# An FFN in split fp32: the forms of its inner activations are stored as two parts in place of one

## The chip, the cores and the metric

The kernel runs on one core of a Trainium2 chip, as one program. Its time is the device time of one execution in microseconds (us), the median of several runs. The core has a tensor engine (PE, whose weight loads are listed as PEld), a vector engine (DVE), a scalar engine (ACT), GpSimd (POOL) and SyncE (SP), from whose queue nearly all DMA transfers of this kernel are issued. Each engine carries out its own instructions in the order in which they stand; engines wait for each other by semaphores. The tensor engine runs at one of two clocks, 1.2 or 2.4 GHz; the profile gives the granted clock as a share of the higher one.

## The reference

One layer of a streaming encoder trunk for two streams of 512 and 32 frames, so 544 columns in all, all in fp32. The mixers ahead of the FFN and the last norm are not touched by the change. What matters here is the FFN with its squared relu:

```python
D_MODEL = 2048
D_FF = 4 * D_MODEL
...
h2 = rmsnorm(x, norm2_g[l])
a = jax.nn.relu(jnp.einsum('btd,df->btf', h2, w_ff1[l]))
x = x + jnp.einsum('btf,fd->btd', jnp.square(a), w_ff2[l])
...
y = rmsnorm(x, final_norm_g)
```

## The kernel before

**Two parts.** The tensor engine takes the type fp32r, a shortened fp32. To keep fp32 accuracy, each operand is split into a high part (a cast to fp32r, by ACT) and a low part (the operand less its high part, by DVE), and each product is made of three matmuls: high x high, high x low, low x high (`product`, lines L1145 to L1147). `split_w` (L109, L110) does this for weight tiles; what it makes is a tile `hl`.

**Seven products for eight.** Both FFN products work on 2 x 2 blocks of the matrices with a scheme of seven products. `seven` runs them in the order X, F, X, C, X, D, E, each into a PSUM bank of its own (`bX`, `bF`, `bC`, `bD`, `bE`). X is made three times; the bank is copied by ACT to C, to D (both L1132) and to E (L1134) on the way, so the second product into bX can start only when the copy to bC is done, and the third after the copy to bD. The right operands of the seven products are seven sums and differences of the four blocks of activations, the *forms* (`forms`, L1103 to L1106: t1, t2, t3, t4; the blocks themselves are the other three).

**First product (w1).** 32 rounds (`for i in range(32)`), of 7 x 8 x 3 = 168 matmuls of 128 x 128 by 272 columns. A round loads four 512 KB weight tiles (a11, a21, a22, a12), makes sums of them and splits them. Behind its products, while the next round's products already run, the round's result goes through relu and square (ACT, L1248 to L1253) and the four form sums (DVE), into one tile `ft` of 7 x 272 columns, which goes to DRAM (`hd`, one tensor per chunk of four rounds) as fp32 in one 952 KB store. In rounds 4 to 19 another step stands there too: a tile `xv` of the residual stream is loaded from `x2`, multiplied by the norm's factors on DVE (L1264) and stored back.

**Second product (w2).** Eight chunks of eight turns, 84 matmuls each. A chunk uses the seven forms of four rounds, so seven tiles `hf` with 4 x 272 columns in each of two parts. `load_form` loads one 544 KB form as fp32 into the second half of its tile, casts the high part into the first half (L1192) and subtracts in place (L1193). The seven forms of the next chunk are loaded in turns 1 to 7 of the one before; those of the first chunk during round 32, one after each of its products (`first_forms`), and of these the last two are split only in the course of turn 1 (`late`, `late_split`). A turn takes two weight tiles, r1 and r2, and makes `s12` and `s34`, sums of their halves, each 128 x 1024, split them, and needs s12 from its second product, F, on. F's carry, `accf`, goes through all chunks; the rest of the sums are added to `acc`, whose 16 tiles are loaded from `x2` in the first chunk.

**What sets the order.** PE's instructions stand as the program writes them in the mixers; else the recording layer orders every engine's instructions by priority and dependences, so an edit can move instructions that the source leaves alone. `self.first()` raises the priority of weight loads, splits and bank copies. `self.after` adds an order without a wait: the splits of later chunks' forms were held behind the copy to accf and the last sum of their turn (`hold`).

Of the kernel before, what the change touches and what calls it, by code (L numbers as in the profile page):

```python
# [7 lines left out]
F32 = mybir.dt.float32  # L8
F32R = mybir.dt.float32r
# [7 lines left out]
HALF = 272  # L17
# [21 lines left out]
class Build:  # L39
# [800 lines left out]
    def run(self):  # L840
        tc, nc = self.tc, self.nc
# [4 lines left out]
        dt = lambda n, shape: self.dr.tile(shape, F32, name=n)  # L846
# [4 lines left out]
        self.hd = [dt(f"hd{i}", [128, 7, 4, HALF]) for i in range(8)]  # L851
# [313 lines left out]
    def ffn(self):  # L1165
# [20 lines left out]
        def load_form(ck, f, hold=None, later=None):  # L1186
            t = h_tile("hf")
            r = t[:, 1].bitcast(F32)
            nc.sync.dma_start(r, self.hd[ck][:, f].rearrange("q j t -> q (j t)"))

            def split():
                c0 = a.copy(t[:, 0], r)  # L1192
                c1 = v.tensor_sub(t[:, 1], r, t[:, 0].bitcast(F32))  # L1193
                if hold:
                    self.after(c0, hold[0], "spread")
                    self.after(c1, hold[1], "spread")

            split() if later is None else later.append(split)
            s = lambda k: slice(HALF * k, HALF * k + HALF)
            return [(t[:, 0, s(k)], t[:, 1, s(k)]) for k in range(4)]  # L1200

        w2 = d["w2"]
        nxt, raws, late = [], [], []

        def first_forms(i):

            nxt.append(load_form(0, i, None, late if i > 4 else None))
            if i == 0:

                self.rings["w"] = [0, self.rings["w"][1][-2::-1]]  # L1210
            if i in (0, 3):
                raws.append(self.load_raw(w2[0, len(raws)]))

        for i in range(32):
# [41 lines left out]
            nc.sync.dma_start(self.hd[ck][:, :, j], ft)  # L1256
# [22 lines left out]

        def late_split(i):  # L1280
            if i in (3, 4):
                late.pop(0)()

        for ck in range(8):
            cur, nxt = nxt, []
            for i in range(8):
# [65 lines left out]
                C, E, D, X, F = self.seven(left, cur, 4, accf[:, i] if ck else None, late_split if ck == i == 0 else lambda p: None)  # L1352
                h0 = a.copy(accf[:, i], F)
                if ck == 7:
                    v.tensor_add(hi, hi, accf[:, i].unsqueeze(1).broadcast_to([128, 2, HALF]))
                for p, o in ((C, lo[:, 0]), (X, hi[:, 1]), (D, hi[:, 0]), (E, lo[:, 1])):
                    h1 = v.tensor_add(o, o, p)
                if ck < 7 and i < 7:
                    nxt.append(load_form(ck + 1, i, (h0.ins.name, h1.ins.name)))
# [153 lines left out]
```

## Time and profile before

| | us |
|---|---|
| median of 3 runs | 2269.75 (2269.53 to 2270.97) |
| the profiled execution | 2272.85 |
| its span, first to last instruction | 2271.1 |
| PE busy | 2227.4, 98% of the span |
| DVE busy | 1807.8, 80% |
| ACT busy | 1284.3, 57% |

The first FFN product runs from 902 to 1569.5 us of the span, the second from there to about 2248. Busy time counts computing instructions only. Matmuls are pipelined: each record lasts some 290 ns, while a new one starts every 126 ns, so progress is read from the starts, and a gap in them from a wait that the timeline shows in brackets, with the instruction that ended it. Times of the timeline are us from the start of the span.

### The profile page before, as it was taken

The numbers are of one execution on the slowest core, as the hardware profiler recorded it, in microseconds if no ns is written. First come the engines' busy times: TensorE is split into PE (matmuls) and PEld (weight loads), VectorE is DVE, ScalarE is ACT, GpSimd is POOL, SyncE is SP. The second block draws the span as 40 slices with busy tenths as digits, with TensorE's granted clock in tenths as the row PEclk, the third lists the DMA queues.
The fourth block names the chain that finished last, engine by engine and source line by source line (L and its number), as shares of the span: only waits on it lengthen the run. The fifth ranks groups of instructions, "written<-read, shape, count | busy, mean of one in ns | idle before, by whom it ended". The sixth has DMA issues, their size and how long they took to land.

```text
span 2271.1 us, 46587 instructions
## 1 busy us (share of the span) xinstructions
PE 2227.4 (98%) x19222; PEld 2207.0 (97%) x19222; DVE 1807.8 (80%) x2951; ACT 1284.3 (57%) x2268; POOL 26.6 (1%) x59
## 2 busy tenths in 40 slices
PE   8999999999999999999999999999999999999997
PEld 8999989999999999999999999999999999999997
DVE  7979989877567478777777777777988888888898
ACT  5656666564655256555555555556565565566574
POOL 0000000000000000000000000000000000000000
PEclk9999999999999999999999999999999999999999
DMA  5222222222345565445545444446454244344332
GB/s 196 89 83 93 89 88 83 86 94 75 117 149 179 161 200 173 148 157 178 171 167 178 169 153 151 142 148 241 175 181 162 100 175 162 99 176 163 104 120 98
DMA packets 141317, 322.04 MB, mean 142 GB/s; under 512 B 13360, under 2 KB 68272, under 8 KB 141104
## 3 DMA queue, kind: packets, MB, share of 16 engines
q1 hardware_dynamic: 138928, 316.83, 42.0%
q8 instruction: 150, 2.46, 0.4%
q10 hardware_dynamic: 2176, 2.23, 0.3%
q14 instruction: 63, 0.52, 0.1%
HBM read 262.14 MB, written 56.87 MB: 140 GB/s over the span
## 4 chain that ended last, share of the span: by engine, by line
PE 88%; DVE 7%; ACT 2%; DMA 1%; issue 1%; SPq 0%; DVEq 0%; ACTq 0%
PE g L125 9%; PE bX L1145 8%; PE bX L1146 8%; PE g L127 8%; PE g L126 8%; PE bX L1147 8%; PE bC L1146 3%; PE bD L1146 3%; PE bC L1145 3%; PE bD L1145 3%; PE bF L1145 3%; PE bF L1146 3%; PE bE L1146 3%; PE bE L1145 3%; PE bD L1147 3%; PE bC L1147 3%
## 5 line engine op out<-in xcount | busy, mean ns | idle before, releaser
L125 PE MATMUL g<-a,hl 128*128 128x272 f32 x1648 | 488.0, 296 | 7.2 <-ACT hl L109 6.3
L127 PE MATMUL g<-a,hl 128*128 128x272 f32 x1648 | 477.6, 290 | 1.5 <-DVE hl L110 1.5
L126 PE MATMUL g<-a,hl 128*128 128x272 f32 x1648 | 476.5, 289 | 0.7 <-DVE a L1006 0.7
L110 DVE TENSOR_TENSOR hl<-w,hl 128x1024 fp32r<-128x1024 f32 (+3 forms) x344 | 379.1, 1111 | 121.0 <-ACT hl L109 120.4
L109 ACT CAST hl<-w 128x1024 fp32r<-128x1024 f32 (+3 forms) x344 | 330.6, 961 | 207.4 <-PE g L127 114.6
L110 DVE TENSOR_TENSOR hl<-s,hl 128x1024 fp32r<-128x1024 f32 x256 | 313.1, 1223 | 107.8 <-ACT hl L109 107.7
L109 ACT CAST hl<-s 128x1024 fp32r<-128x1024 f32 x256 | 268.8, 1050 | 177.9 <-PE bD L1147 95.0
L125 PEld LDWEIGHTS g<-a,hl 128*128 128x128 f32 x1648 | 313.3, 190 | 9.6 <-ACT hl L109 6.5
L127 PEld LDWEIGHTS g<-a,hl 128*128 128x128 f32 x1648 | 312.6, 190 | 2.4 <-DVE hl L110 2.4
L126 PEld LDWEIGHTS g<-a,hl 128*128 128x128 f32 x1648 | 312.6, 190 | 1.7 <-DVE a L1006 0.9
L1145 PE MATMUL bX<-hf,hl 128*128 128x272 f32 x768 | 222.5, 290 | 0.5 <-ACT bD L1132 0.5
L1146 PE MATMUL bX<-hf,hl 128*128 128x272 f32 x768 | 222.7, 290 | 0.0
L1146 PE MATMUL bX<-f,hl 128*128 128x272 f32 x768 | 222.6, 290 | 0.0
L1145 PE MATMUL bX<-f,hl 128*128 128x272 f32 x768 | 222.1, 289 | 0.3 <-ACT hl L109 0.3
L1147 PE MATMUL bX<-f,hl 128*128 128x272 f32 x768 | 221.5, 288 | 0.7 <-DVE hl L110 0.7
L1147 PE MATMUL bX<-hf,hl 128*128 128x272 f32 x768 | 221.4, 288 | 0.0
L1145 PEld LDWEIGHTS bX<-hf,hl 128*128 128x128 f32 x768 | 144.8, 189 | 0.9 <-ACT bD L1132 0.7
L1147 PEld LDWEIGHTS bX<-f,hl 128*128 128x128 f32 x768 | 144.6, 188 | 1.0 <-DVE hl L110 1.0
L1145 PEld LDWEIGHTS bX<-f,hl 128*128 128x128 f32 x768 | 144.7, 188 | 0.5 <-ACT hl L109 0.5
L1146 PEld LDWEIGHTS bX<-hf,hl 128*128 128x128 f32 x768 | 144.6, 188 | 0.0
L1147 PEld LDWEIGHTS bX<-hf,hl 128*128 128x128 f32 x768 | 144.5, 188 | 0.0
L1146 PEld LDWEIGHTS bX<-f,hl 128*128 128x128 f32 x768 | 144.4, 188 | 0.0
(437 smaller groups left out, 5731.8 us busy)
## 6 DMA issues: line engine op xcount, KB each, us to landing
w<-w SPq DMA_DIRECT2D x256, 512.0 KB, 3.8
w<-wi SPq DMA_DIRECT2D x76, 512.0 KB, 3.3
hd<-ft SPq DMA_DIRECT2D x32, 952.0 KB, 4.6
hf<-hd SPq DMA_DIRECT2D x56, 544.0 KB, 6.4
w<-wo SPq DMA_DIRECT2D x32, 512.0 KB, 3.8
x<-x SPq DMA_DIRECT2D x32, 272.0 KB, 2.8
hhl<-hh SPq DMA_DIRECT2D x16, 274.0 KB, 3.5
x<-xT SPq DMA_DIRECT2D x16, 272.0 KB, 5.2
```

The costliest lines, as they stand in the source:

```text
L109: self.nc.scalar.copy(hi[:, cols], w[:, cols])
L110: self.last_lo = self.nc.vector.tensor_sub(lo[:, cols], w[:, cols], hi[:, cols].bitcast(F32)).ins.name
L125: te.matmul(o, wh, xh, start=k == 0, stop=False)
L126: te.matmul(o, wh, xl, start=False, stop=False)
L127: te.matmul(o, wl, xh, start=False, stop=k == nk - 1)
L1145: te.matmul(o, wh[:, s], xh, start=start and k == 0, stop=False, skip_group_check=True)
L1146: te.matmul(o, wh[:, s], xl, start=False, stop=False, skip_group_check=True)
L1147: te.matmul(o, wl[:, s], xh, start=False, stop=k == nk - 1, skip_group_check=True)
```

## The change

The forms are split once, in the round that makes them, and stored as two parts. A round casts its whole tile of seven forms to `fh` (ACT, 128 x 1904), subtracts in place (DVE, 128 x 1904) and makes two 952 KB stores, one for each part. `hd` is twice as large. `load_form` is one DMA of 1088 KB and nothing else; the two late splits of the first chunk and the held order of the others go with the splits.

```diff
@@ -848,7 +848,7 @@
         self.ud = [dt(f"ud{i}", [128, 4, NC5]) for i in range(8)]
         self.hh = [dt(f"hh{i}", [128, 4, NC5 - 1]) for i in range(8)]
         self.x2 = [dt(f"x2{i}", [128, T]) for i in range(NK)]
-        self.hd = [dt(f"hd{i}", [128, 7, 4, HALF]) for i in range(8)]
+        self.hd = [dt(f"hd{i}", [128, 7, 2, 4, HALF]) for i in range(8)]
         ones = self.pp.tile([128, 128], F32, name="ones")
         nc.gpsimd.memset(ones, 1.0)
         self.c["ones"] = ones
@@ -1183,28 +1183,18 @@
                 self.hslots.insert(keep, slot)
             return self.hp.tile([128, 2, 4, HALF], F32R, tag=slot, name=n).rearrange("q a k t -> q a (k t)")
-        def load_form(ck, f, hold=None, later=None):
+        def load_form(ck, f):
             t = h_tile("hf")
-            r = t[:, 1].bitcast(F32)
-            nc.sync.dma_start(r, self.hd[ck][:, f].rearrange("q j t -> q (j t)"))
-
-            def split():
-                c0 = a.copy(t[:, 0], r)
-                c1 = v.tensor_sub(t[:, 1], r, t[:, 0].bitcast(F32))
-                if hold:
-                    self.after(c0, hold[0], "spread")
-                    self.after(c1, hold[1], "spread")
-
-            split() if later is None else later.append(split)
+            nc.sync.dma_start(t.bitcast(F32), self.hd[ck][:, f].rearrange("q a j t -> q a (j t)"))
             s = lambda k: slice(HALF * k, HALF * k + HALF)
             return [(t[:, 0, s(k)], t[:, 1, s(k)]) for k in range(4)]
         w2 = d["w2"]
-        nxt, raws, late = [], [], []
+        nxt, raws = [], []
         def first_forms(i):
-            nxt.append(load_form(0, i, None, late if i > 4 else None))
+            nxt.append(load_form(0, i))
             if i == 0:
                 self.rings["w"] = [0, self.rings["w"][1][-2::-1]]
@@ -1253,7 +1243,13 @@
                 a.activation(z, z, AF.Square)
             t = iter((1, 2, 4, 6))
             self.forms((h11, h12, h21, h22), lambda: ft[:, next(t)])
-            nc.sync.dma_start(self.hd[ck][:, :, j], ft)
+
+            fh = tp.tile([128, 7, HALF], F32R, tag="fh", name="fh", bufs=1)
+            fl = ft.bitcast(F32R)
+            a.copy(fh, ft)
+            v.tensor_sub(fl, ft, fh.bitcast(F32))
+            for n, z in enumerate((fh, fl)):
+                nc.sync.dma_start(self.hd[ck][:, :, n, j], z.bitcast(F32))
             if i == 1:
                 self.after(v.tensor_add(self.acc, self.acc, self.rb), last_sum, "start of the products first")
@@ -1276,10 +1272,6 @@
         def end_tile(slot, n):
             t = self.hp.tile([128, 2, 4, HALF], F32R, tag=slot, name=n)
             return t.rearrange("q a k t -> q (a k t)")
-
-        def late_split(i):
-            if i in (3, 4):
-                late.pop(0)()
         for ck in range(8):
             cur, nxt = nxt, []
@@ -1349,14 +1341,14 @@
                     for m in range(2):
                         v.tensor_add(self.acc[:, HALF:T], self.acc[:, HALF:T], sq[:, m])
                     continue
-                C, E, D, X, F = self.seven(left, cur, 4, accf[:, i] if ck else None, late_split if ck == i == 0 else lambda p: None)
-                h0 = a.copy(accf[:, i], F)
+                C, E, D, X, F = self.seven(left, cur, 4, accf[:, i] if ck else None)
+                a.copy(accf[:, i], F)
                 if ck == 7:
                     v.tensor_add(hi, hi, accf[:, i].unsqueeze(1).broadcast_to([128, 2, HALF]))
                 for p, o in ((C, lo[:, 0]), (X, hi[:, 1]), (D, hi[:, 0]), (E, lo[:, 1])):
-                    h1 = v.tensor_add(o, o, p)
+                    v.tensor_add(o, o, p)
                 if ck < 7 and i < 7:
-                    nxt.append(load_form(ck + 1, i, (h0.ins.name, h1.ins.name)))
+                    nxt.append(load_form(ck + 1, i))
                 if ck == 7:
                     for j in range(2):
                         sq = sqt() if i or j else self.acc
```

The change moves instructions that it does not name. The rows below are read as line, operation, out<-in and shape, in the order in which they stand on the engine; line numbers of the second fence of each pair are those of the changed kernel, in which L1239 is L1249 of before (relu), L1243 is L1253 (square), L1293 to L1299 are L1301 to L1307 (the sums to s12 and s34), L1188 is L1189 (load of a form), L1252 is L1256 (the store) and L1308 is L1316 (load of acc).

ACT at the start of a round of the first product, before, from the square of the previous round's h12 on; `bE` is the previous round's last bank and `bC<-bX` is the copy that the round's second X waits for:

```order
L1253 ACTIVATE h_14510<-h_14510 128x272
L1249 ACTIVATE ft<-bE 128x272
L109 CAST hl<-s 128x1024
L1253 ACTIVATE ft<-ft 128x272
L1132 COPY bC<-bX 128x272
L109 CAST hl<-w 128x1024
L109 CAST hl<-s 128x1024
```

The same place after:

```order
L1243 ACTIVATE h_14554<-h_14554 128x272
L1239 ACTIVATE ft<-bE 128x272
L109 CAST hl<-s 128x1024
L1243 ACTIVATE ft<-ft 128x272
L1249 CAST fh<-ft 128x1904
L1132 COPY bC<-bX 128x272
L109 CAST hl<-w 128x1024
```

The new cast of the seven forms stands between the last square and the copy to bC; it does so in all 32 rounds.

DVE at the change-over from the first product to the second, before, from the sum to h12 of round 32 on (`s<-w` and `s<-s,w` of 512 columns are the sums to s12, then to s34):

```order
L1247 TENSOR_TENSOR h_19214<-bD,fsb 128x272
L1301 TENSOR_TENSOR s<-w 128x512
L1193 TENSOR_TENSOR hf<-hf 128x1088
L1302 TENSOR_TENSOR s<-s,w 128x512
L1103 TENSOR_TENSOR ft<-h_19214,ft 128x272
L1105 TENSOR_TENSOR ft<-ft,h_19214 128x272
L1104 TENSOR_TENSOR ft<-ft 128x272
L1306 TENSOR_TENSOR s<-w 128x512
L1106 TENSOR_TENSOR ft<-ft 128x272
L110 TENSOR_TENSOR hl<-s,hl 128x1024
L1307 TENSOR_TENSOR s<-w,s 128x512
```

The same place after:

```order
L1237 TENSOR_TENSOR h_19328<-bD,fsb 128x272
L1103 TENSOR_TENSOR ft<-h_19328,ft 128x272
L1105 TENSOR_TENSOR ft<-ft,h_19328 128x272
L1104 TENSOR_TENSOR ft<-ft 128x272
L1106 TENSOR_TENSOR ft<-ft 128x272
L1250 TENSOR_TENSOR ft<-ft,fh 128x1904
L1293 TENSOR_TENSOR s<-w 128x512
L1298 TENSOR_TENSOR s<-w 128x512
L1294 TENSOR_TENSOR s<-s,w 128x512
L110 TENSOR_TENSOR hl<-w,hl 128x512
L1299 TENSOR_TENSOR s<-w,s 128x512
L110 TENSOR_TENSOR hl<-s,hl 128x1024 x2
```

The sums to s12 stood among the form sums and the splits of loaded forms; now they stand behind all form sums and the new wide subtraction. On PE, turn 1 now runs its product C before its F.

SP at the same change-over, before (`hd_100` holds the forms of the first chunk, `hd_101` those of the second, `hd_107` those of the last; `x_84` and on are tiles of x2):

```order
L89 DMA w<-w 128x1024
L1189 DMA hf<-hd_100 128x1088 x3
L1189 DMA hf<-hd_101 128x1088
L89 DMA w<-w 128x1024
L1189 DMA hf<-hd_101 128x1088 x2
L1256 DMA hd_107<-ft 896x1x272
L89 DMA w<-w 128x1024 x2
L1316 DMA acc_19237<-x_84 128x544
L1316 DMA acc_19237<-x_85 128x544
```

The same place after:

```order
L89 DMA w<-w 128x1024
L1188 DMA hf<-hd_100 128x2176 x3
L1252 DMA hd_107<-fh 896x1x272
L1252 DMA hd_107<-ft 896x1x272
L1188 DMA hf<-hd_101 128x2176
L1308 DMA acc_19355<-x_84 128x544
L1308 DMA acc_19355<-x_85 128x544
L89 DMA w<-w 128x1024
```

The weight tile r2 of turn 2, the second `w<-w` of each fence, stood ahead of the last round's store; now it stands behind both stores, a form and two loads of acc. The tile acc lies in memory that `ft` and `fh` leave.

## Rows read from the trace of the kernel before

**Rows 1.** Busy time by stretch: stretch, its length, each engine's busy us, clock, DMA.

```profile
core 0: us, PE busy (x) PEld busy (x) DVE busy (x) ACT busy (x) POOL busy (x), PEclk, DMA share, GB/s
1250.00:1400.00 150.00, 150.00 (x1191) 150.00 (x1190) 112.25 (x127) 80.35 (x136) 0.00 (x0) 1.00 0.48 160
1700.00:1900.00 200.00, 200.00 (x1586) 200.00 (x1585) 174.02 (x243) 119.03 (x186) 0.00 (x0) 1.00 0.40 139
```

**Rows 2.** Waits, 902 to 2200: who, for whom, us in all, times, longest.

```profile
PE bF L1145 <- ACT hl L109: 2.5, 1, 2.5
PE bX L1145 <- ACT bD L1132: 0.5, 1, 0.5
DVE xv L1264 <- DMA xv<-x: 16.6, 15, 2.3
```

**Rows 3.** Timeline of the change-over, PE, then ACT: start, duration, instruction [idle before].

```profile
1569.57 0.29 PE L1145 MATMUL bX<-hf,hl 128*128 128x272 f32 x1
...
1570.94 0.29 PE L1147 MATMUL bX<-hf,hl 128*128 128x272 f32 x1
1573.71 0.39 PE L1145 MATMUL bF<-hf,hl 128*128 128x272 f32 x1 [2.48 <-ACT hl L109]
...
1580.53 0.39 PE L1145 MATMUL bX<-hf,hl 128*128 128x272 f32 x1 [0.46 <-ACT bD L1132]
...
1585.16 0.29 PE L1145 MATMUL bX<-hf,hl 128*128 128x272 f32 x1
...
1572.62 1.04 ACT L109 CAST hl<-s 128x1024 fp32r<-128x1024 f32 x1
```

**Rows 4.** Busy time of the 3 us behind the first gap, columns as rows 1.

```profile
1574.00:1577.00 3.00, 3.00 (x15) 3.00 (x15) 3.00 (x5) 0.00 (x0) 0.00 (x0) 0.50 0.42 143
```

**Rows 5.** Groups of both FFN products: count, busy us, mean ns, idle before.

```profile
L1192 ACT CAST hf<-hf 128x1088 fp32r<-128x1088 f32 x56 | 62.0, 1107 | 3.3 <-DMA hf<-hd 3.3
L109 ACT CAST hl<-w 128x512 fp32r<-128x512 f32 x64 | 39.9, 624 | 10.9 <-PE bC L1147 5.8 <-PE bX L1147 3.1
...
L1193 DVE TENSOR_TENSOR hf<-hf 128x1088 fp32r<-128x1088 f32 x56 | 72.0, 1286 | 2.9 <-ACT hf L1192 2.9
L110 DVE TENSOR_TENSOR hl<-w,hl 128x512 fp32r<-128x512 f32 x64 | 43.8, 685 | 1.9 <-ACT hl L109 1.9
```

**Rows 6.** Timeline of one round of the first product, PE, then ACT.

```profile
1208.86 0.29 PE L1145 MATMUL bX<-f,hl 128*128 128x272 f32 x1
...
1211.90 0.29 PE L1145 MATMUL bF<-f,hl 128*128 128x272 f32 x1
...
1214.92 0.29 PE L1145 MATMUL bX<-f,hl 128*128 128x272 f32 x1
...
1217.94 0.29 PE L1145 MATMUL bC<-f,hl 128*128 128x272 f32 x1
...
1212.10 0.37 ACT L1132 COPY bC<-bX 128x272 f32<-128x272 f32 x1 [1.37 <-PE bX L1147]
1212.38 1.05 ACT L109 CAST hl<-w 128x1024 fp32r<-128x1024 f32 x1
```

**Rows 7.** Timeline of DVE in that round and the next.

```profile
1208.18 0.73 DVE L1264 TENSOR_TENSOR xv<-xv,rb 128x544 f32<-128x544 f32 x1 [1.70 <-DMA xv<-x]
...
1213.28 0.43 DVE L1106 TENSOR_TENSOR ft<-ft 128x272 f32<-128x272 f32 x1
...
1227.83 0.73 DVE L1264 TENSOR_TENSOR xv<-xv,rb 128x544 f32<-128x544 f32 x1 [0.16 <-DMA xv<-x]
...
1232.94 0.44 DVE L1106 TENSOR_TENSOR ft<-ft 128x272 f32<-128x272 f32 x1
```

**Rows 8.** Timeline of SP's DMA issues ahead of the change-over.

```profile
1565.89 0.33 SPq L89 DMA_DIRECT2D w<-w  x1
```

**Rows 9.** DMA traffic of 1551 to 1571; busy time of one microsecond in it.

```profile
DMA packets 2541, 7.26 MB, mean 363 GB/s; under 512 B 189, under 2 KB 1085, under 8 KB 2539
...
1569.00:1570.00 1.00, 1.00 (x10) 1.00 (x9) 1.00 (x2) 1.00 (x2) 0.00 (x0) 1.00 1.12 416
```

**Rows 10.** Weight tiles w in 1700 to 2000: time from issue to landing.

```profile
DMA to landing us min/median/max: 3.0/4.1/6.4
```

## The prediction

> **What bounds the kernel now.** I read the table of stretches first. In the 150 us from 1250, inside the first FFN product, PE issues 1191 matmuls, one per 126 ns, at full clock; in the 200 us from 1700, inside the second, 1586, again 126 ns; both stretches are 100% busy [rows 1]. The table of waits then says what interrupts it: over 1300 us of FFN, PE waits twice, 2.5 us and 0.5 us [rows 2]. So from 902 to 2200 matmuls set the end, with one flaw, the change-over between the two products: the first turn's X begins at 1569.57, the second turn's at 1585.16, 15.59 us for 84 matmuls that cost 84 x 0.126 = 10.6 us [rows 3]. Of the 5.0 us lost, 2.64 are the gap from the last matmul of X (1570.94 + 0.13) to F at 1573.71, 0.5 the second wait, and the rest, 1.8 us, goes at a granted clock of 0.50, that is 1.2 GHz, which follows the long gap: 15 matmuls in the 3 us from 1574, 0.20 us each [rows 3, 4].
>
> **What it removes.** 56 casts on ACT of 1.107 us and 56 subtractions on DVE of 1.286 us, 62 and 72 us [rows 5]. The splits of 49 forms, seven chunks of seven, lie inside the second product, where PE never waits for either engine; there this buys nothing. PE cannot go below 126 ns per matmul and the change removes no matmul. Only the change-over could gain, at most the 5.0 us.
>
> **What it adds to each round of the first product.** One cast of 1904 columns on ACT, one subtraction of 1904 on DVE, a second 952 KB store. No such width stands in the trace; from 512 to 1088 columns ACT goes from 0.624 to 1.107 us and DVE from 0.685 to 1.286 [rows 5], so 0.84 and 1.04 ns a column: 1.107 + 816 x 0.00084 = 1.79 us and 1.286 + 816 x 0.00104 = 2.14 us, both as estimates from these rows. Engine time is there (ACT and DVE are busy 80 and 112 of 150 us [rows 1]); place is the question.
>
> The cast needs the last form, t4 (L1106), and the order puts it, in all 32 rounds, right before the copy bC<-bX. That copy must be done before the round's third product (X again) may overwrite bX. Take the round whose X begins at 1208.86: F begins at 1211.90, the second X at 1214.92 [rows 6]. Before, the copy ran from 1212.10 to 1212.47, 2.4 us early. Now: t4 ends 1213.28 + 0.43 = 1213.71 [rows 7]; cast to 1215.50; the next ACT instruction starts about 0.1 us before the last one's end (1212.38 against 1212.47 [rows 6]), so the copy runs from 1215.4 to 1215.8, and PE starts X a moment later, at about 1215.85. **PE waits 0.9 us** where it never waited.
>
> How late t4 is depends on xv, the x2 tile that rounds 4 to 19 rescale: DVE waits for its DMA in order, and the forms stand behind it. In the shown round DVE sat 1.70 us for it; in the next round only 0.16, and t4 was done by 1233.38 [rows 7], 1.5 us earlier against its round's start (21.2 us later). t4 moves one for one with that wait, and 1.70 gives 0.9 too late, so a wait up to 0.80 is free. The table has 15 such waits, 16.6 us, mean 1.11, longest 2.3 [rows 2]. If all were the mean: 15 x 0.31 = 4.6 us; if spread evenly from 0.16 to 2.3, the part over 0.80 averages 1.5 x 1.5 / 2 / 2.14 = 0.53, times 16 = 8.4. I take **7 us**, nearer to the spread, since the two rows shown lie far apart. Bounds: 0 if all land like that 0.16, 16 x 1.5 = 24 if all like the longest. The other 16 rounds have no xv, so t4 comes no later than after the 0.16, and cost nothing.
>
> Behind the cast, DVE: the subtraction ends about 1217.65, the low half of w(a12) 1.14 later, 1218.8; its product C, pushed from 1217.94 [rows 6] to 1218.85, needs it in its third matmul, 1219.1. It just fits. SP: the two stores are issued after cast and subtraction, at about 1216 and 1218, and the weight loads behind them move back by some 2 us; they are for two rounds later, so free. The doubled store adds 1 MB to 3.7 MB a round (six or seven 512 KB loads and one store before), on DMA engines busy half the time [rows 1].
>
> **The change-over, first turn (+3 us).** Here the cast and subtraction of round 32 stand ahead of what turn 1 needs, s12 and its split. Before, DVE computed s12 between two of the removed subtractions and ACT cast it at 1572.62 [rows 3]; the removed work was part of the wait. Now: E of round 32 ends about 1569.7; relu, square and t4 at 0.43 each: 1571.0; cast to 1572.7; subtraction to 1574.8; three sums of 512 columns at 0.6 to 1576.6; cast of s12, 1.05, to 1577.6: F may start at 1577.7, against 1573.71. PE has one product to put in between, C, after its copy (1573.0), to 1574.5. The low half of s12, behind two more short instructions on DVE, comes at 1578.95, and F's third matmul needs it: with X, C and two matmuls done, 58 remain, to 1578.95 + 7.3 = 1586.25 at full clock, 1.1 us later than 1585.16. The gap before F, 3.1 us, is longer than the 2.64 that ended at half clock, so I add the 1.8 us again: 2.9, about +3. Bounds -2 (s12's sums are ready earlier than worked out) and +5.
>
> **Second turn (+2 us).** Its weight tile r2 was issued at 1565.89 [rows 8]; now SP has it behind both stores of round 32, a form, and two acc loads that reuse the store's memory and so wait for its landing. In this stretch the DMA engines are full: 363 GB/s on average over 1551 to 1571, 416 in the microsecond from 1569 [rows 9]. Forms 1 to 6 follow the second store of round 31, issued some 7 us after that round's end (as the 1216 to 1218 above), about 1555.2: 0.98 + 6 x 1.11 + 0.52 = 8.2 MB, 19.7 us at 416 GB/s, and 2 us until landing (of the shortest load's 3.0 us [rows 10], 512 KB take 1.3 at that rate): 1577. The last stores, 1.95 MB, then reach 1581.6, the form 1584.3, acc and r2 1587. F of turn 2 wants its s12 three microseconds after its X, at 1586.25 + 1.8 + 3 = 1591.1; 1587 + 1.8 for the sums + 1.05 for the cast gives 1589.9, and the low half 0.7 more, 1590.6: nothing lost. At 363 GB/s r2 lands at 1591: 3.5 us lost. I take 2, between the two, bounds 0 and 6.
>
> **The later chunk borders.** Seven forms are fetched per border, 7.8 MB instead of 3.9, among weights that before took 3.0 to 6.4 us to land, 4.1 in the middle [rows 10]. SP's new order lets a weight load pass after every one or two forms at first, where it had three forms in a row, so I put 0; bounds -1 and +12, 2 us at each of six.
>
> **Sum.** 7 + 3 + 2 = 12.0 us on the profiled execution's 2272.85, 2284.85. That execution is 3.1 us above the median of the runs, 2269.75; on the median's scale: **2281.8 us**.
>
> **Rivals.** (a) *The clock goes with every wait.* Before, the 2.64 us gap was followed by half clock and another 1.8 us [rows 3, 4]; the wait of 0.5 us by none. The waits forecast in the rounds lie between, up to 1.5 us. If eight of them each cost 1.8 more: +14.4, 2297. The Trainium skill has this rule (TensorE: Matmul & The Clock Gate, Part 1: The HAM clock gate): an array that idles is gated to half its clock, and activity releases it; the trace agrees for the long gap, and shows none of this for the short one. (b) *DMA is the bound at the borders.* If weights queue behind doubled forms: +12 there, +4 more at the change-over, 2298. It decides if a weight lands later than some 6 us after issue; before, the slowest took 6.4, the middle one 4.1 [rows 10]. (c) *Faster.* xv early, so no wait in the rounds, and at the change-over the freed 2.4 us per form on DVE and ACT count for more than the one late pair: the whole 5.0 us flaw goes, 2264.8. It decides if s12 is ready by 1571.1. The order of DVE, the wide subtraction first, speaks against it. (d) *No difference.* The waits in the rounds stay under 2 us in sum and the change-over breaks even: 2270 to 2274. That the splits are not really gone is excluded: their rows are missing from the new order.
>
> **How the numbers follow.** 0.2% of 2270, 4.5 us, is about what a measurement can tell from no change. Forecast (2275 to 2290): 0.58. (a) 0.09. (b) 0.12. (c) 0.06. (d) 0.15. Slower is forecast, (a) and (b): 0.79. The range 2272 to 2298 takes in (a), (b) and half of (d); left out are (c), the rest of (d) and some tail.
>
> **What would show it.** In the changed profile: PE waits at X for the copy to bC in rounds 4 to 19, at most 1.5 us each, some 7 us in all, none in the other rounds; some 18.5 us from X of turn 1 to X of turn 2 (10.6 before any wait), with the gaps at C and F, and a wait at F of turn 2; 126 ns per matmul elsewhere; no half clock outside the change-over. No wait at bC, or one in rounds without xv, would make the first term wrong; a second turn that starts F at once, the last.

## The result, and the profile after

| | before | after |
|---|---|---|
| median | 2270.36 (2269.53 to 2271.32, 4 runs) | 2299.26 (2296.53 to 2300.43, 4 runs) |
| profiled execution | 2272.85 | 2296.53 |
| span | 2271.1 | 2294.7 |

The change makes the kernel **slower, ratio 1.0129 (95% interval 1.0114 to 1.0143)**, 28.9 us by the medians. Forecast were 2281.8 us, with a range of 2272 to 2298: the direction was right, the size was under half, and the time lies 1.3 us above the range.

Where it went is read from the starts of X on PE in both traces, round by round and turn by turn. From X of one round (or turn) to X of the next, with the profiled execution of each kernel:

| stretch | before | after | difference | forecast |
|---|---|---|---|---|
| start of the span to X of round 2 (911.12, 907.98) | 911.1 | 908.0 | -3.1 | 0 |
| rounds 2 to 31 | 637.0 | 652.9 | +15.9 | +7 |
| round 32 | 21.5 | 21.2 | -0.3 | 0 |
| turn 1 | 15.60 | 19.08 | +3.5 | +3 |
| turn 2 | 10.62 | 16.79 | +6.2 | +2 |
| turn 3 | 10.60 | 11.56 | +1.0 | 0 |
| the other 61 turns | | | +0.1 | 0 |
| end | | | +0.4 | 0 |

So the mixers, which the change doesn't touch, ran 3.1 us shorter in the profiled execution of after than in that of before (the first product's first matmul starts at 888.4 us before and at 885.2 after; in the other traces X of round 2 lies from 908.5 to 912.3), and the FFN is 26.3 us longer. Two places hold all of this: the 16 rounds behind an xv step, 1.0 us each, and the first three turns, 10.6 us.

The stretches of the changed kernel, with the columns of [rows 1]:

```profile
core 0: us, PE busy (x) PEld busy (x) DVE busy (x) ACT busy (x) POOL busy (x), PEclk, DMA share, GB/s
...
902.00:1250.00 348.00, 339.40 (x2664) 336.57 (x2663) 283.76 (x303) 206.05 (x317) 0.00 (x0) 1.00 0.62 204
1250.00:1400.00 150.00, 146.82 (x1157) 145.94 (x1157) 121.85 (x129) 90.11 (x139) 0.00 (x0) 1.00 0.62 200
1400.00:1560.00 160.00, 160.00 (x1270) 160.00 (x1269) 130.53 (x135) 98.48 (x152) 0.00 (x0) 1.00 0.60 195
1560.00:1620.00 60.00, 50.24 (x358) 48.26 (x356) 36.14 (x49) 26.54 (x40) 0.00 (x0) 0.94 0.94 357
...
1700.00:1900.00 200.00, 200.00 (x1587) 200.00 (x1586) 155.48 (x228) 104.63 (x170) 0.00 (x0) 1.00 0.52 184
```

PE was 100% busy in both products before; now it idles up to 1400, stands still a sixth of the time around the change-over, and is full everywhere else, at 126 ns per matmul. In the second product DVE is busy 155 us of 200 where it was 174, and ACT 105 where it was 119: the removed splits did go, and nothing came of it. The DMA engines, which move 200 GB/s in place of 160 in the rounds, are 94% busy in the 60 us of the change-over.

Its waits (columns as in [rows 2]; the first and third of 905 to 1562, the second of 1560 to 1720), and the two new groups (columns as in [rows 5]):

```profile
PE bX L1145 <- ACT bC L1132: 11.8, 16, 1.3
...
PE bF L1145 <- ACT hl L109: 5.2, 2, 3.0
...
DVE xv L1260 <- DMA xv<-x: 26.4, 16, 2.2
```

```profile
L1250 DVE TENSOR_TENSOR ft<-ft,fh 128x1904 fp32r<-128x1904 f32 x32 | 68.5, 2142 | 24.5 <-ACT fh L1249 24.5
L1249 ACT CAST fh<-ft 128x1904 fp32r<-128x1904 f32 x32 | 57.2, 1786 | 66.5 <-DVE ft L1106 66.5
```

The wait at bC came 16 times, in the 16 rounds that follow an xv step, and in no other round: the mechanism of the forecast. But DVE's waits for xv, on which it hangs, are no longer 16.6 us in sum, as in [rows 2], but 26.4.

One round of the changed kernel, the one whose X begins at 1216.04, against [rows 6, 7]: PE, ACT and DVE, then SP's load of the next xv and the X that begins the next round:

```profile
1216.04 0.29 PE L1145 MATMUL bX<-f,hl 128*128 128x272 f32 x1
...
1222.43 0.39 PE L1145 MATMUL bX<-f,hl 128*128 128x272 f32 x1 [0.16 <-ACT bC L1132]
...
1220.30 1.79 ACT L1249 CAST fh<-ft 128x1904 fp32r<-128x1904 f32 x1 [2.41 <-DVE ft L1106]
1222.00 0.38 ACT L1132 COPY bC<-bX 128x272 f32<-128x272 f32 x1
...
1214.73 0.72 DVE L1260 TENSOR_TENSOR xv<-xv,rb 128x544 f32<-128x544 f32 x1 [1.08 <-DMA xv<-x]
...
1219.84 0.43 DVE L1106 TENSOR_TENSOR ft<-ft 128x272 f32<-128x272 f32 x1
...
1231.73 0.42 SPq L1259 DMA_DIRECT2D xv<-x  x1
...
1237.67 0.29 PE L1145 MATMUL bX<-f,hl 128*128 128x272 f32 x1
```

The chain is there link by link: xv's multiplication starts 1.08 us late, t4 stands 5.1 us behind it, the cast starts when t4 ends (1220.27) and takes 1.79, the copy to bC runs from 1222.00 to 1222.38, and X starts at 1222.43, 6.39 us after the round's first X where it was 6.06 [rows 6]. The round as a whole took 21.63 us (1216.04 to 1237.67), 0.43 more than before.

The change-over of the changed kernel, against [rows 3, 8]: PE, DVE, then SP:

```profile
1582.02 0.29 PE L1145 MATMUL bX<-hf,hl 128*128 128x272 f32 x1
...
1585.70 0.39 PE L1145 MATMUL bC<-hf,hl 128*128 128x272 f32 x1 [2.01 <-ACT bC L1132]
...
1590.47 0.39 PE L1145 MATMUL bF<-hf,hl 128*128 128x272 f32 x1 [3.00 <-ACT hl L109]
...
1601.10 0.29 PE L1145 MATMUL bX<-hf,hl 128*128 128x272 f32 x1
...
1607.22 0.39 PE L1145 MATMUL bF<-hf,hl 128*128 128x272 f32 x1 [2.19 <-ACT hl L109]
...
1585.40 2.14 DVE L1250 TENSOR_TENSOR ft<-ft,fh 128x1904 fp32r<-128x1904 f32 x1 [1.84 <-ACT fh L1249]
1587.46 0.68 DVE L1293 TENSOR_TENSOR s<-w 128x512 f32<-128x512 f32 x1
...
1604.14 0.69 DVE L1293 TENSOR_TENSOR s<-w 128x512 f32<-128x512 f32 x1 [1.28 <-DMA w<-w]
...
1587.57 0.51 SPq L1252 DMA_DIRECT2D hd<-ft  x1
1588.17 3.44 SPq L1188 DMA_DIRECT2D hf<-hd  x1
1598.13 0.80 SPq L1308 DMA_DIRECT2D acc<-x  x2
1598.97 0.43 SPq L89 DMA_DIRECT2D w<-w  x1
```

In turn 1, F waits for s12, whose sums start when the wide subtraction ends (1587.46). In turn 2, F waits for s12 again, and there the sums start when r2 has landed (1604.14); r2 was issued at 1598.97, behind the first two loads of acc, which SP could issue only at 1598.13, 10.6 us after the last store, which had landed after 10.4. Before, the same distance (1574.62 to 1581.51 on SP) was 6.9 us, and r2 stood ahead of it.

### The profile page after: what moved, and what is told of

It reads as the page before. It is cut to its first block, busy times and chain, and to the rows that moved or that the text cites. A ratio compares the mean times of both kernels' runs of the same rounds, so it can differ in the third digit from the quotient of the medians.

```text
span 2294.7 us, 46558 instructions
## 1 busy us (share of the span) xinstructions
PE 2232.0 (97%) x19222; PEld 2207.3 (96%) x19222; DVE 1805.9 (79%) x2927; ACT 1287.5 (56%) x2244; POOL 26.3 (1%) x59
## 4 chain that ended last, share of the span: by engine, by line
PE 73%; DVE 14%; DMA 5%; issue 4%; ACT 3%; SPq 0%; DVEq 0%; ACTq 0%
PE g L125 9%; PE g L127 8%; PE g L126 8%; PE bX L1145 6%; PE bX L1146 6%; PE bX L1147 6%; DVE hl L110 5%; DMA xv<-x 4%; PE bF L1147 2%; PE bC L1146 2%; PE bC L1145 2%; PE bD L1146 2%; PE bD L1145 2%; PE bF L1146 2%; PE bF L1145 2%
## 5 line engine op out<-in xcount | busy, mean ns | idle before, releaser
L1145 PEld LDWEIGHTS bX<-f,hl 128*128 128x128 f32 x768 | 144.7, 188 | 15.9 <-ACT bC L1132 15.3
```

Of the source, the lines that this page charges most:

```text
L1145: te.matmul(o, wh[:, s], xh, start=start and k == 0, stop=False, skip_group_check=True)
```

## The experiments

All of them are read by two numbers beside the time: what rounds 2 to 31 take more than 636.98 us (X of round 2 to X of round 32, changed kernel +15.9), and what the change-over takes more than the 662.7 us of before (X of round 32 to X of turn 61, where the shortened turns of the end begin; changed kernel +10.5).

### Rounds: is it the place of the cast?

**Without xv.** The `if 4 <= i < 20` block of the changed kernel is left out.

> The changed kernel without the xv step: rounds 4 to 19 no longer load, rescale and store their x2 tile (so the residual stream keeps a wrong scale; nothing else is left out). Theory 1 (the copy to bC stands behind the cast of the seven forms, and that cast is late only because DVE waited for xv): no wait of PE at X for bC in any round; rounds 4 to 19 take 21.20 us each as the other rounds do, about 16 us less in all, some 2283 us. Rival (the second store's traffic, or the cast itself, costs the time): rounds 4 to 19 stay near 22.2 us, or rounds without xv would have shown the loss too; some 2298 us.

Measured: rounds +0.0, change-over +9.3, 2282.27 us. The stretch of 1250 to 1400 is full again, with the cast, the subtraction and the second store all in it:

```profile
1250.00:1400.00 150.00, 150.00 (x1190) 150.00 (x1190) 123.59 (x129) 92.79 (x143) 0.00 (x0) 1.00 0.58 190
```

Theory 1 holds: in the rounds neither the cast nor the second store's traffic costs anything by itself (the load and the store of xv, 272 KB each, are gone here, too).

**The cast behind the copy.** Same instructions, another place, and a buffer of its own for xv:

```diff
-            a.copy(fh, ft)
-            v.tensor_sub(fl, ft, fh.bitcast(F32))
...
+                c0 = a.copy(fh, ft)
+                c1 = v.tensor_sub(fl, ft, fh.bitcast(F32))
+                if i < 31:
+                    self.after(c0, self.bc, "behind the copy")
+                    self.after(c1, self.last_lo, "behind the weights")
...
-                x = tp.tile([128, 7, HALF], F32, tag="ft", name="xv", bufs=2).rearrange("q f t -> q (f t)")[:, 0:T]
+                x = tp.tile([128, T], F32, tag="xv", name="xv", bufs=1)
```

(the split of a round is written into the next round's products; `self.bc` is the copy to bC there, `self.last_lo` the low half of a12).

> The changed kernel with the cast of the seven forms ordered behind the next round's copy to bC, and the subtraction behind the low half of a12; xv gets a buffer of its own, so that the later stores hold up no other tile. The same instructions, the same traffic. Theory 1: the rounds go back to 21.20 us although xv is waited for as before (20 to 30 us in sum on DVE); about 16 us less, some 2283 us. Rival (traffic or engine time costs the rounds): no gain, some 2298 us.

Measured: rounds +0.1, change-over +10.1, 2282.53 us. ACT in the round that begins at 1208.44:

```profile
1211.68 0.37 ACT L1132 COPY bC<-bX 128x272 f32<-128x272 f32 x1 [1.38 <-PE bX L1149]
1211.96 1.05 ACT L109 CAST hl<-w 128x1024 fp32r<-128x1024 f32 x1
1212.91 1.79 ACT L1252 CAST fh<-ft 128x1904 fp32r<-128x1904 f32 x1
```

The 15.9 us are gone. But the edit moved more than the cast: the subtraction stands later, too, and with a buffer of its own xv is issued 12 to 21 us ahead of the next round's X in 11 of the 16 rounds, not 6, so that the waits for xv are 8.1 us in sum and not the expected 20 to 30. Five of them, of 1.2 to 3.0 us, were left. In the changed kernel such a wait costs PE its length less 0.65 us (worked out in the account of the prediction), 4.9 us for these five; here they moved PE by 0.1 in all. For them the place of the cast is shown to be the cause; in the other 11 rounds no wait is left that could show it. The runs together do show it: with the waits for xv and without the cast (the kernel before, 16.6 us of waits) PE waits nowhere in the rounds, with the cast and without the waits (no xv) nowhere either, and with both the rounds lose 15.9 us.

**The cast twice.** `a.copy(fh, ft)` stands there two times.

> The changed kernel with the cast of the seven forms made twice (1.7 us more on ACT in each of 32 rounds, in front of the copy to bC). Theory 1: the 16 rounds with xv, which already wait, grow by the whole 1.7 us, 27 us; the other rounds, which have some 1.3 us in hand, wait 0.4 us each, 5 us; the change-over grows by up to 1.7; some 2330 us. Rival (ACT is idle 4 of 10 us, so a cast hides): under 5 us more.

Measured: rounds +27.0, change-over +10.3, 2309.97 us: in the rounds 11.1 us more than in the changed kernel, where 32 were expected. The recording layer put the copy to bC *between* the two casts, and the second one delays what comes behind it instead: a12's split and the copy to bD. Nearly every round loses some 0.85 us, with xv or without (waits for xv are 2.5 us here, since its load had moved ahead by one weight load). So this run says only that ACT's idle time doesn't hide a cast that stands in front of a copy; as a test of 1.7 us per round it failed, since the dose changed the order.

### Rounds: why did the waits for xv grow?

**Two stores before.** The kernel before with each store made twice.

> The kernel before, with each round's 952 KB store made twice (the second into a tensor that nobody reads), so it has the changed kernel's store traffic and no other part of the change. If the growth of DVE's waits for xv (16.6 us before, 26.4 us after) comes from the traffic and from SP's queue, they grow here too, to 20 to 30 us, while PE still waits nowhere in rounds 2 to 31 and the time stays within 3 us of before, up to what the change-over adds. Rival (the stores slow PE): rounds 4 to 19 grow by up to 1 us each, 16 us.

Measured: rounds 0.0, change-over -0.3, 2272.78 us (span 2271.0, before 2271.1). The waits for xv did not grow: first line below, 15.2 us. The expectation that the stores' traffic makes them grow fell.

**The second store off SP's queue.** The changed kernel with `(nc.gpsimd if n and i < 31 else nc.sync).dma_start(...)`.

> The changed kernel with the store of the low parts issued from GpSimd's DMA queue in rounds 1 to 31, so that the weight loads and the load of xv no longer stand behind it on SP; the cast stays in front of the copy to bC. Theory 4 (the waits for xv grew because the weight loads, and with them xv, start later on SP and meet a backlog): DVE's waits for xv fall from 26.4 to 16 to 20 us, and rounds 4 to 19 lose 6 to 10 us in all in place of 15.8. Rival (the bytes themselves slow xv's landing): the waits stay at 24 to 28 us and the loss at 14 to 17 us.

Measured: rounds +15.1, change-over +10.6, 2296.58 us. The waits stay at 25.5 us, second line: the place behind the second store isn't the cause either. The rival's numbers came, but its cause, the bytes, does not fit the other runs: with the stores twice the waits are 15.2 us, and with all the new bytes in the kernel before (next section) 16.4.

```profile
DVE xv L1266 <- DMA xv<-x: 15.2, 16, 1.7
```

```profile
DVE xv L1260 <- DMA xv<-x: 25.5, 16, 2.4
```

What is seen: the 16 loads of xv are issued 6.16 us ahead of the next round's X before and 5.95 after (the rows above: 1231.73 to 1237.67), and their multiplication starts 4.82 us behind the issue before and 5.21 after. These 0.6 us, 16 times, are the growth. With the stores twice the two numbers are 6.11 and 4.67; with the second store on GpSimd's queue 5.68 and 4.89. Why a load of the same size takes 0.4 us longer in the changed kernel **stays open**.

The sum also differs from run to run. In three experiments of the next section the rounds stand in the changed kernel's order, and lose 18.9, 15.1 and 17.5 us, with waits for xv of 29.4, 23.5 and 28.0 us. By this some 2 us of the 28.9 between the medians that the two profiled executions don't show are no surprise.

### Change-over: places or bytes?

One caution goes for this whole part. Each trace is one execution, and the granted clock is at half for a different time in each: of the time from X of round 32 to X of turn 4, 3.4 us before, 6.8 in the changed kernel, 13.6 in two of the runs below. About 3.3 us of it cost some 1.4 us (the two lines under the first chunk in fp32), so a difference of 1 or 2 us between two runs need not come from the edit.

**s12 first.** Turn 1's s12 is written into round 32, and round 32's split is ordered behind it:

```diff
+            if i == 31:
+                self.after(c0, order[0], "weights first")
+                self.after(c1, order[1], "weights first")
```

> The changed kernel with one reordering at the change-over: the cast and the subtraction of round 32 are ordered behind turn 1's s12 and its split; no DMA is moved. Its three turns from X of turn 1 to X of turn 4 took 47.4 us in the changed kernel (36.8 before, 31.8 without any wait). Theory 2 (two bounds in a row: turn 1 waits for the sums behind the wide subtraction, but turn 2 waits for its r2, whose issue stands behind the last stores' landing): turn 1 shortens by 2 to 4 us to some 15 to 17, turn 2 grows by as much or more, since the store is now issued later; the sum of the three turns stays between 46 and 48.5 us. Rival (the place of the wide subtraction on DVE is the whole cause): the sum falls to some 40 to 43 us.

Measured: turn 1 15.80, turn 2 20.08, turn 3 11.56, together 47.4 as in the changed kernel; change-over +10.7. What turn 1 gains (3.3) turn 2 loses (3.3), since its copy to bC now waits for the first sum into acc:

```profile
1608.37 0.59 PE L1145 MATMUL bC<-hf,hl 128*128 128x272 f32 x1 [3.58 <-ACT bC L1132]
...
1607.42 0.44 DVE L1361 TENSOR_TENSOR acc<-acc,bC 128x272 f32<-128x272 f32 x1 [6.33 <-DMA acc<-x]
```

**r2 of turn 2 ahead of the stores.** `if i in (0, 3):` becomes `(0, 3, 5, 6)` in `first_forms`.

> The changed kernel with turn 2's two weight tiles asked for in round 32, so that r2 of turn 2 stands on SP ahead of the last round's stores, as it did before; DVE and ACT keep their order in turn 1. Theory 2: turn 1 stays at 18 to 20 us, turn 2 falls from 16.8 to under 12 us; the three turns take 41 to 43 us, the kernel 4 to 6 us less than the changed one. Rival (the DMA engines are full, so r2 lands late wherever it stands, or the forms do): three turns at 46 us or more.

Measured: turns of 19.31, 11.78 and 12.24, together 43.3; change-over +6.5, 2293.13 us. Theory 2 holds for the two turns that it spoke of: turn 2 gains 5.0 us, of which 0.7 are lost again in turn 3 and 0.2 in each of turns 1 and 4, so that the three turns lie 0.3 us above its 41 to 43.

**Both r2 early.** `(0, 1, 5, 6)`; the order then puts s12 ahead of the wide subtraction.

> As the run before, and also r2 of turn 1 asked for two products earlier, ahead of the forms 3 to 7; with it the order puts turn 1's s12 ahead of round 32's wide subtraction on DVE. Theory 2: both gaps close; turn 1 takes 11 to 14 us, turn 2 11 to 13, the three turns 33 to 38 us, no longer than the 36.8 of before. What could be late next is the last forms, 1.1 MB each, which landed up to 18 us after their issue. Rival (the doubled forms and stores fill the DMA engines, and something of them is always late): over 42 us.

**With the split of the rounds behind the copy as well.**

> The order edits together: the split of the rounds behind the copy to bC (as in the second run, with xv in a buffer of its own) and the early r2 of turns 1 and 2. If the two theories add up: rounds of 21.20 us, three turns of 33 to 38 us, and a time within 4 us of the kernel before. Rival (what one edit gains the other loses, since the later stores of round 31 and 32 meet the forms): three turns of 42 us or more, 6 us or more above before.

Measured: three turns of 44.7 and 43.4 us, change-over +8.3 and +6.6 (2298.37 and 2279.46 us; the second has its rounds at +0.0). Both miss the 33 to 38 that theory 2 wanted and lie where the rivals had them. Of its waits, those of turn 1 at C and F are gone; turn 2's F still waits, 2.1 and 1.5 us, since its r2, now issued 6.6 and 3.5 us ahead of turn 1's X, lands only 18.7 and 15.4 us later. Behind it stands the load of acc, which waits for the last store's landing: as with s12 first, turn 2's copy to bC comes late, 4.0 us in both. Places alone do not close the gap, so theory 2 is not the whole.

**Every form loaded twice, in the kernel before,** and then **every store twice as well**: the new bytes, with the splits of before.

> The kernel before with every form loaded twice (the second time into the half that the cast then overwrites): the loads move as many bytes as the changed kernel's, the stores and all the splits are those of before. Its order on SP comes out like the changed kernel's at the change-over: r2 of turn 2 behind the last store, a form and two loads of acc. Theory 3 (at the change-over it is the bytes: the forms of the first chunk fill the DMA engines, the last store lands late behind them, and r2 and acc stand behind that store): the rounds stay at 21.20 us, the three turns from X of turn 1 grow from 36.8 to 42 us or more, and the later chunk borders stay without a loss; 5 to 10 us more than before. Rival (the place of the new cast and subtraction on ACT and DVE): the three turns stay under 38 us.

> The kernel before with every form loaded twice and every round's store made twice: all the bytes of the changed kernel, with the splits and their places of before. From X of round 32 to X of turn 4 the kernel before takes 58.3 us, with doubled stores alone 57.9, with doubled loads alone 63.8, the changed kernel 68.6. Theory 3a (bytes are all of it): 66.5 to 69 us here. Theory 3b (bytes are half of it, and the other half is the wide cast and subtraction of round 32 standing ahead of turn 1's sums): 62.5 to 65.5 us. The rounds stay at 21.20 us in both.

Measured: change-over +5.6 and +11.6, rounds 0.0 in both; 2277.79 and 2282.34 us. X of round 32 to X of turn 4 takes 63.8 and 69.5 us, the second half a microsecond above the 66.5 to 69 of theory 3a. SP behind the last store, in the first and in the second of these kernels:

```profile
1571.31 0.53 SPq L1257 DMA_DIRECT2D hd<-ft  x1
...
1579.19 0.80 SPq L1317 DMA_DIRECT2D acc<-x  x2
1580.04 0.42 SPq L89 DMA_DIRECT2D w<-w  x1
```

```profile
1571.06 1.81 SPq L1259 DMA_DIRECT2D hdd<-ft  x1
...
1584.08 0.80 SPq L1319 DMA_DIRECT2D acc<-x  x2
1584.92 0.43 SPq L89 DMA_DIRECT2D w<-w  x1
```

From the last store to the first load of acc: 6.9 us before, 7.9 with the loads doubled, 13.0 with both, 10.6 in the changed kernel. The new bytes, with the order on SP that the recording layer makes of them (r2 behind the store, here as in the changed kernel), are enough for a loss of the changed kernel's size at the change-over, without the new cast and subtraction. It takes both: doubled loads alone cost 5.6, doubled stores alone nothing. That it is the same loss is not shown. In the second kernel 2.9 us of PE's waits, read from the starts (start to start less 0.126), are at turn 1's C for splits of loaded forms, which the changed kernel no longer has, and its clock is at half for 13.6 us in place of 6.8. How the 10.5 us of the changed kernel divide between the bytes and the place of the new cast and subtraction stays open.

**The last stores on ACT's queue.**

```diff
+                    (nc.scalar if i >= 31 else nc.sync).dma_start(self.hd[ck][:, :, n, j], z.bitcast(F32))
```

> The changed kernel with the rounds' split behind the copy to bC, r2 of turn 2 asked for in round 32, and the two stores of round 32 issued from ACT's DMA queue instead of SP's, where they stand behind seven forms. Theory 3: those stores land in some 5 to 7 us instead of 10, the loads of acc start that much sooner; turn 1 stays near 19 us (its r2 is as late as before), turn 2 10.6 to 11.5 and turn 3 10.6: three turns of 40 to 41 us, 2275 to 2279 us in all. Rival (the queue does not matter, the engines are full): landing after 10 us, turn 3 above 12 as in the run with r2 alone, three turns of 43 us or more.

Measured: three turns of 45.7 us, change-over +9.8, 2284.64 us: a miss. The two stores' time from issue to landing, with r2 of turn 2 early and SP's queue, here, and with the split behind the copy, both r2 early and SP's queue:

```profile
DMA to landing us min/median/max: 11.7/12.0/12.3
```

```profile
DMA to landing us min/median/max: 11.0/11.3/11.6
```

```profile
DMA to landing us min/median/max: 9.7/10.0/10.3
```

Against the first, ACT's queue gains 0.7 us; against the third, which has its rounds split in the same place as this run, it loses 1.3. So no gain of another queue is shown, and the copy to accf on ACT now waits 4.6 us for the store. The rival's landing and sum came (its turn 3 above 12 did not, 11.7), which fits its reading that the engines, which both queues share, are full. So the Trainium skill has it too (DMA: Bandwidth & Descriptors, Queues, rings and completion order): the queues of SP and ACT run on the same DMA engines.

**The first chunk in fp32.** Rounds 1 to 4 store fp32, and their forms are split on load as before; the other seven chunks are as changed, with the cast behind the copy. And the same with the last stores on ACT's queue.

> The changed kernel with the rounds' split behind the copy to bC, and the first chunk left as it was before the change (its four rounds store fp32 forms, which are split on load); the seven other chunks are stored as two parts. Theory 3: without the doubled forms at the change-over r2 and the last store land some 5 us sooner and the order on DVE is again the sums first: rounds of 21.20 us, three turns of 36 to 40 us, a time from 2 us below to 4 us above before. Rival (the doubled stores of the last rounds alone make the gap): three turns of 42 us or more, 6 us or more above before.

> As the run before, with the two stores of round 32 on ACT's DMA queue. Theory 3: at most 2 us less than the run before, where the loads of acc were still late, else the same within 0.5 us. Rival (ACT's stores hold up its casts in turn 1): 1 to 3 us more.

Measured: 2276.71 us (6 runs; ratio to before 1.0032, 1.0021 to 1.0044) and 2279.77 us (4 runs; 1.0044, 1.0027 to 1.0060); rounds 0.0 in both, change-over +5.6 and +7.5, three turns of 39.1 and 43.1. In the first the turns are those of theory 3, the time is not: 7.0 us above before, and not at most 4. Halving the bytes of the first chunk gives back half of the loss, but 3.3 of the 5.6 us now lie in round 32, where the split on load stands in front of other work. These 3.3 are not the edit alone: in the second kernel, with the same order on PE there, round 32 loses 1.2. PE has short waits there in both; behind them the clock fell in the first (first line) and not in the second:

```profile
1562.30:1565.60 3.30, 3.30 (x17) 3.30 (x16) 1.08 (x1) 0.00 (x0) 0.00 (x0) 0.50 1.03 414
```

```profile
1562.30:1565.60 3.30, 3.30 (x28) 3.30 (x28) 2.05 (x3) 0.97 (x3) 0.00 (x0) 1.00 1.04 412
```

That is 17 matmuls in place of 28, and 11 x 0.126 = 1.4 us. In the second kernel ACT's stores hold up its copies, as its rival said. The two stores' time from issue to landing, in the first and in the second:

```profile
DMA to landing us min/median/max: 4.5/4.9/5.3
```

```profile
DMA to landing us min/median/max: 13.3/13.4/13.4
```

Only their queue was edited, but with it SP, which no longer stands at the stores, issues two forms beside them, and the first store, issued 1.0 us ahead of these forms, lands behind both. Why it does stays open. No version here beats the kernel before.

## Why the prediction was right or wrong, point by point

- **What bounds the kernel, and what the removed splits are worth.** Right. PE stays at 126 ns per matmul in the second product with or without 49 splits, and only the change-over could have gained; it didn't.
- **Costs of the new instructions.** Right: 1.786 and 2.142 us, where 1.79 and 2.14 had been worked out from the narrower rows [rows 5].
- **The wait at bC, its place, and the rounds it comes in.** Right, and shown: without xv or with the cast behind the copy it is gone.
- **Its size, 7 us.** Wrong, 15.9. The step that failed is the one that took the waits for xv from the trace of before, as if the change left them alone. With those waits, each less 0.80, the 16 rounds do give 6.9. The threshold was a little high: 0.65 fits the shown round (1.08 less the 0.43 lost), 8.2 in sum. The rest, 7.7 us, is that the waits themselves grew by 0.6 us each: 26.4 - 16 x 0.65 = 16.0, against 15.9 measured. Why they grew stays open. The upper bound of 24 held the value, but the range took in only a part of it.
- **Turn 1, +3.** Near: 3.5, with gaps at C and F as worked out. The reason given holds for the turn: with the sums moved ahead of the wide subtraction it takes 3.3 us less. It does not hold for the end: turn 2 takes these 3.3 us back, and the three turns take 47.4 us either way.
- **Turn 2, +2, at most 6.** Wrong: 6.2, and 1.0 more in turn 3. When r2 would land was well placed: 1591 at 363 GB/s had been the late end; it was 1604.14, and less the 12.45 us by which turn 1 began later, that is 1591.7 (partly by luck: the sum had it queue behind bytes, in the run it was issued only when the last store had landed, and took 5.1 us more). The step that failed here is the choice of the middle between the full rate and this; in a stretch whose DMA engines are full the late end was the one to take. Left out, too, was that this wait also brings half clock: read from the starts, the 16.79 us are 10.6 of work, 4.2 of waits (2.35 at F and three of some 0.6) and some 2.0 at the lower clock. And nothing was said of the loads of acc as the next thing late, though their place behind the store was seen.
- **The later borders, 0.** Right, 0.1. The rival that put 12 us there (b) was wrong in its place; its DMA bound is real, but only where forms, the last stores and acc come together; that its 2298 lies next to the measured time is luck.
- **Rival (a), the clock at every wait.** Did not come: the clock is 1.00 from 902 to 1560, with 16 waits in it.
- **The traffic of a round.** Misread, in a place on which nothing rests: a round loads four weight tiles, not six or seven; with its store and the two transfers of xv these are the 3.6 MB, near the 3.7 given.

In sum 12 were forecast and the FFN lost 26.3; of the difference 8.9 are the rounds and 5.6 the first three turns.

## What to carry to other kernels

Work that is cheap and has room on its engine can still cost up to its length if it stands in front of a short instruction that another engine waits for: here one copy; the cure is an order, not less work. If a term hangs on a wait that the trace of before shows, do not take that wait over as it is: ask what the change does to its releaser. And moving work out of one stage by storing more bytes is paid for where loads and stores of neighbouring stages meet, in the order that larger transfers make the recording layer choose; a reordering that removes the first wait there shows the next one.

## What the runs showed of the hardware

A full DMA stretch delays what stands in it far more than its own bytes. In the changed kernel's change-over, with the DMA engines 94% busy, a 512 KB weight issued at 1572.62 landed after 11.4 us and the last 952 KB store after 10.4; in the whole program the middle ones take 4.2 and 5.7. With both r2 early, such a weight took 18.7 us.

The clock, in the changed kernel (columns as in [rows 1]):

```profile
1586.00:1589.00 3.00, 1.48 (x12) 1.26 (x11) 3.00 (x4) 0.62 (x1) 0.00 (x0) 1.00 1.02 418
1591.50:1594.00 2.50, 2.26 (x10) 2.26 (x11) 1.38 (x2) 0.13 (x1) 0.00 (x0) 0.53 1.10 360
1610.00:1613.00 3.00, 2.78 (x15) 2.56 (x13) 0.16 (x1) 0.57 (x2) 0.00 (x0) 0.64 1.07 439
```

Right after the wait of 2.0 us at C it is still full; after the second, of 3.0 us at F, it is half; and after the 2.2 us at turn 2's F, which follows two waits of 0.46 us, it falls again. Sixteen waits of up to 1.3 us, one per round, left it at full speed. The length of a single wait does not decide it: in the run without xv the same wait of 2.0 us at C is followed by half clock,

```profile
1571.80 0.39 PE L1145 MATMUL bC<-hf,hl 128*128 128x272 f32 x1 [2.01 <-ACT bC L1132]
```

```profile
1572.30:1575.00 2.70, 2.24 (x11) 1.92 (x9) 2.70 (x4) 0.42 (x1) 0.00 (x0) 0.50 1.02 403
```

and in round 32 of the first kernel with the first chunk in fp32 it is half behind three waits of 0.1, 0.5 and 0.7 us.
